# Queries and output gate as seven of eight block products, and the gates' tiles moved into the attention

## The chip, the core and the metric

The kernel runs on one core of one Trainium2 chip. Its metric is the device time of one execution in microseconds. The engines are named as in the profile: PE is TensorE (matmul), PEld its weight load, DVE VectorE, ACT ScalarE, POOL GpSimd, SP SyncE. SP and POOL each issue DMAs on a queue of their own.

## The reference

One layer of a hybrid encoder: 512 tokens, width 1024, float32. What bears on the change, with `rmsnorm(h)` the normalised input:

```python
h = rmsnorm(x, norm_mix_g)
gq, gk, gv, gr, glr, fq, fk, fv, ff, g_gla, g_fox = jnp.split(h @ w_in, IN_OFFSETS, axis=-1)
o_gla = gla_chunked(gq, gk, gv, log_a)                     # 4 heads of 128
o_gla = rmsnorm(o_gla, gla_out_norm_g) * silu(gr)          # output gate gr: 512 columns
fqh, fkh = rmsnorm(fq, fox_q_norm_g), rmsnorm(fk, fox_k_norm_g)   # 8 heads of 64
o_fox = fox_attention(fqh, fkh, fv, log_f)                 # causal softmax attention
y = sigmoid(g_gla + gate_b[0]) * (o_gla @ w_gla_branch) \
    + sigmoid(g_fox + gate_b[1]) * (o_fox @ w_fox_branch)
x = x + y @ w_out
a, val = jnp.split(rmsnorm(x, norm_ffn_g) @ w_up, 2, axis=-1)
return x + (gelu(causal_dwconv(a)) * val) @ w_down         # and a last rmsnorm
```

## The kernel before, in words

Every large product is made with float32 operands as a high and a low half: a piece of weights (128 x 1024) is loaded into a raw tile (`raw`, `rawz`, `rawp`, `rawx` by place), ACT casts it to `wh` (line 293), DVE makes `wl`, the difference (line 294), and PE runs three matmuls for each of its blocks: high by high, high by low, low by high (`mm3`, lines 328 to 330). Pieces are split three ahead of their use (`NW`). `recipes` is the list of pieces in order of use; `then` says what a split sets off: a plain load on SP's queue, or an accumulating load on POOL's queue, which adds a second block of weights to a raw tile. `COPY_AT` and `ADD_AT` hang DMAs in DRAM onto pieces: 24 copies and 24 accumulating additions that build sums of the down projection's blocks (`wsum`).

Some products are split in 2 x 2 blocks and made with seven block products instead of eight (numbered 1 to 7, in the order 5, 1, 3, 6, 2, 7, 4 or like it). Their weights are single blocks or sums of blocks, which the accumulating loads form: product 6 takes the raw tile of product 5 with a block added, 4 that of 6, 7 that of 3. In before this holds for keys and values (`fox_kv`, 14 half pieces of 12 matmuls, two steps each), the out product, the up and the down projection.

The stages, in order of PE: narrow products and the first sums, GLA's values (`vg`, 4 pieces), `fox_q` (4 pieces of 24 matmuls, 512 columns), `fox_kv`, with the steps of gated linear attention put between; then the forgetting attention; then eight branches; then out, up and down products.

Work that can be put between other work is a generator in `work`; `fill(n)` takes n steps of it. In the attention the generators are gate tiles (`gate_tile`): one step is one k of eight, three matmuls. There are 12 of them: 4 of the output gate (`zr`) and 8 of the first merge gate (`zg`). `FRONT` and `RUNS` set the order by hand: for each pair of units (`unit`: two heads and one or two blocks of queries) the logits are made (line 983), then a number is so many steps of gate tiles, `k` prepares keys and queries of the next two heads (`kh`, `kl`, `qh`, `ql`), `t` transposes a unit's probabilities (line 1017; ACT casts to `ph`, line 1023, DVE makes `pl`, line 1024), and `v` multiplies them with the values (line 1042). Behind the logits stand a DVE reduction (`ISA`, line 990), the exponential (ACT, line 995), the reciprocal and the scaling (ACT, line 997), then `t`.

The 8 tiles of the second gate (`zf`) alternate with the branches, two ahead (`GAHEAD`). A branch c is 24 matmuls (`pg` and `pf`), two sigmoids, two multiplies on DVE (lines 1157 and 1158), an addition on POOL (lines 1161 and 1168), and the making of the out product's operands (`o1`, `o7` for c < 4, `o65`, `o3`, `o24` for c >= 4), on ACT and DVE.

Of the kernel before, what the change touches and what calls it, by code (L numbers as in the profile page):

```python
# [53 lines left out]
GAHEAD = 2  # L54
# [39 lines left out]
def hybrid_kernel(ctx: ExitStack, tc, xT, xt, wp, wu, wd, wf, wn, pp, aw2, fing, out):  # L94
# [55 lines left out]
    at_pair = {}  # L150
    for p, r in PAIR:
        k11, k21, k12, k22 = (wps[i + r] for i in (12, 14, 8, 10))
        new, before, place = {
            1: (k11, None, "rawz"), 2: (k21, None, "rawz"), 3: (k22, None, "rawp"), 7: (k12, 3, None),
            5: (k12, None, "raw"), 6: (k22, 5, None), 4: (k21, 6, None),
        }[p]
        at_pair[p, r] = len(recipes)
        recipes.append((new, at_pair[before, r] if before else None, 1024, place))
# [519 lines left out]
    def fox_q():  # L678
        ssq = gpool.tile([P, NT, FH], F32, name="qssq")

        def done(tt, ps):
            nc.scalar.activation(out=qf[:, tt, :], in_=ps, func=AF.Copy, scale=rt[:, tt : tt + 1])
            squares(qf, ssq, tt)

        yield from token_group(xh, xl, done)
        qk_norm(qf, ssq, range(NT))

# [1129 lines left out]
```

## Time and profile before

| | |
|---|---|
| median of three runs | 688.78 us (688.37 to 690.36) |
| profiled execution | 688.75 us |
| its span | 687.0 us |
| mean granted clock of TensorE | 0.999 |
| DMA traffic | 142.23 MB, mean 207 GB/s |

Spans and starts are in microseconds from the start of the span. A row of the timeline has the start, the duration, engine, line, operation, what it writes and reads, and in brackets how long the engine was idle and what ended that. A row of the windows gives the busy time of each engine in that stretch, with the number of instructions, then the granted clock, the share of the 16 DMA engines that was busy and GB/s.

### The profile page before, as it was taken

How to read it: one execution, taken by the hardware profiler on the slowest of the kernel's cores; microseconds unless marked ns; L12 is line 12 of the kernel's file. 1: busy time of each engine (PE TensorE's matmuls, PEld its weight loads, DVE VectorE, ACT ScalarE, POOL GpSimd, SP SyncE). 2: the span in 40 equal slices, each digit the busy share in tenths (PEclk: the TensorE clock that was granted, in tenths of full speed). 3: DMA queues.
4: the chain of work that ended last, by engine and by line, in shares of the span. 5: the costliest groups of instructions: out<-in, count | busy, mean ns of one | idle time of the engine just before them, and what ended most of it. 6: DMA issues, size and time to landing. Idle time of an engine off the chain costs nothing.

```text
span 687.0 us, 10636 instructions
## 1 busy us (share of the span) xinstructions
PE 680.2 (99%) x3875; PEld 585.4 (85%) x3875; DVE 547.8 (80%) x856; ACT 430.9 (63%) x698; POOL 136.3 (20%) x196
## 2 busy tenths in 40 slices
PE   9999999999999999999999999999999999999996
PEld 6788888888888888888888999999999999888885
DVE  7774988858776767687679999888998889977884
ACT  8487676677767744344584956655666666655663
POOL 1125110122321424331210221121122111000222
PEclk9999999999999999999999999999999999999999
DMA  8769488989765489967975898999999988866643
GB/s 310 270 192 306 99 273 221 311 196 217 178 140 122 119 248 199 281 147 213 213 253 133 158 211 210 228 228 223 196 201 214 204 202 254 268 209 173 196 139 122
DMA packets 46184, 142.23 MB, mean 207 GB/s; under 512 B 5396, under 2 KB 9388, under 8 KB 46004
## 3 DMA queue, kind: packets, MB, share of 16 engines
q1 hardware_dynamic: 31156, 92.98, 40.3%
q0 software_dynamic: 11808, 43.52, 35.8%
q10 hardware_dynamic: 3168, 5.05, 2.1%
q8 instruction: 30, 0.49, 0.3%
q14 instruction: 22, 0.18, 0.1%
HBM read 137.32 MB, written 27.28 MB: 240 GB/s over the span
## 4 chain that ended last, share of the span: by engine, by line
PE 99%; ACT 0%; issue 0%; DVE 0%; ACTq 0%
PE ps_mm L328 21%; PE ps_mm L330 20%; PE ps_mm L329 20%; PE ps_wide L1463 8%; PE ps_wide L328 5%; PE ps_wide L329 5%; PE ps_wide L330 5%; PE ps_wide L1465 4%; PE ps_lg L1042 1%; PE ps_lg L983 1%; PE ps_pt L1017 1%; PE ps_mm L490 1%; PE ps_ax L328 1%; PE ps_ax L330 1%; PE ps_ax L329 1%; PE ps_ax L378 1%
## 5 line engine op out<-in xcount | busy, mean ns | idle before, releaser
L293 ACT CAST wh<-rawx 128x1024 fp32r<-128x1024 f32 x75 | 76.0, 1013 | 61.5 <-PE ps_mm L329 30.9
L328 PE MATMUL ps_mm<-xw,wh 128*128 128x512 f32 (+1 forms) x320 | 109.4, 342 | 0.2 <-ACT wh L293 0.2
L329 PE MATMUL ps_mm<-xw,wh 128*128 128x512 f32 (+1 forms) x320 | 107.8, 337 | 0.0
L330 PE MATMUL ps_mm<-xw,wl 128*128 128x512 f32 (+1 forms) x320 | 107.6, 337 | 0.0
L294 DVE TENSOR_TENSOR wl<-rawx,wh 128x1024 fp32r<-128x1024 f32 x75 | 88.3, 1179 | 13.8 <-ACT wh L293 13.8
L294 DVE TENSOR_TENSOR wl<-raw,wh 128x1024 fp32r<-128x1024 f32 x58 | 74.6, 1287 | 9.7 <-ACT wh L293 9.4
L293 ACT CAST wh<-raw 128x1024 fp32r<-128x1024 f32 x58 | 60.7, 1049 | 32.0 <-PE ps_mm L329 20.2
L328 PEld LDWEIGHTS ps_mm<-xw,wh 128*128 128x128 f32 x320 | 60.8, 190 | 7.8 <-issue 1.2
L330 PEld LDWEIGHTS ps_mm<-xw,wl 128*128 128x128 f32 x320 | 60.8, 190 | 6.5
L329 PEld LDWEIGHTS ps_mm<-xw,wh 128*128 128x128 f32 x320 | 60.8, 190 | 5.9 <-DVE xw L1252 0.2
L294 DVE TENSOR_TENSOR wl<-rawz,wh 128x1024 fp32r<-128x1024 f32 x31 | 39.2, 1266 | 16.7 <-ACT wh L293 16.4
L1463 PE MATMUL ps_wide<-xo,wh 128*128 128x512 f32 x192 | 48.1, 392 | 0.0
L301 POOL DMA_DIRECT2D rawx<-in_wu_dram x30 | 25.9, 865 | 104.6 <-DVE wl L294 68.6
L328 PE MATMUL ps_mm<-xc,wh 128*128 128x256 f32 (+1 forms) x136 | 45.1, 332 | 0.0
L329 PE MATMUL ps_mm<-xc,wh 128*128 128x256 f32 (+1 forms) x136 | 44.6, 328 | 0.0
L330 PE MATMUL ps_mm<-xc,wl 128*128 128x256 f32 (+1 forms) x136 | 44.5, 327 | 0.0
L293 ACT CAST wh<-rawz 128x1024 fp32r<-128x1024 f32 x31 | 32.4, 1044 | 14.2 <-issue 5.0
L1463 PEld LDWEIGHTS ps_wide<-xo,wh 128*128 128x128 f32 x192 | 34.6, 189 | 6.2
L328 PE MATMUL ps_mm<-wh,xw 128*128 128x512 f32 x96 | 37.7, 393 | 0.0
L329 PE MATMUL ps_mm<-wl,xw 128*128 128x512 f32 x96 | 37.4, 390 | 0.0
L330 PE MATMUL ps_mm<-wh,xw 128*128 128x512 f32 x96 | 37.4, 390 | 0.0
L309 POOL COPY tick<-wl 128x1 f32<-128x1 f32 x37 | 10.6, 286 | 134.5 <-DVE wl L294 134.5
(492 smaller groups left out, 1783.6 us busy)
## 6 DMA issues: line engine op xcount, KB each, us to landing
rawx<-in_wu_dram POOLq DMA_DIRECT2D x40, 512.0 KB, 7.1
rawz<-in_wp_dram SPq DMA_DIRECT2D x30, 512.0 KB, 4.6
raw<-in_wp_dram SPq DMA_DIRECT2D x22, 512.0 KB, 5.1
wsum<-in_wd_dram SPq DMA_DIRECT2D x20, 512.0 KB, 6.3
rawx<-in_wu_dram SPq DMA_DIRECT2D x20, 512.0 KB, 4.9
raw<-in_wu_dram SPq DMA_DIRECT2D x20, 512.0 KB, 5.5
rawx<-wsum SPq DMA_DIRECT2D x12, 512.0 KB, 4.0
wsum<-in_wd_dram POOLq DMA_DIRECT2D x10, 512.0 KB, 8.2
```

Source lines behind the costliest of these rows:

```text
L293: nc.scalar.copy(out=hi[:, :m], in_=raw[:, :m])
L294: last_split[:] = [nc.vector.tensor_sub(out=lo[:, :m], in0=raw[:, :m], in1=hi[:, :m].bitcast(F32))]
L301: nc.gpsimd.dma_start(raw, recipes[i][0], accum_op=ALU.add)
L309: now = nc.gpsimd.tensor_copy(out=tick, in_=lo[:, 0:1].bitcast(F32))
L328: mm(ps, lhsT=ah, rhs=bh, start=start, stop=False, **k)
L329: mm(ps, lhsT=ah, rhs=bl, start=False, stop=False, **k)
L330: mm(ps, lhsT=al, rhs=bh, start=False, stop=stop, **k)
L378: mm(warm, lhsT=nc.const_aps.tensor(1.0, (P, P), BF16), rhs=nc.const_aps.tensor(1.0, (P, T), BF16), start=True, stop=True,)
L490: mm(first[i], lhsT=w[:, i * P : (i + 1) * P], rhs=x, start=(k == j == 0), stop=False)
L983: last = mm(lg[:, place_of_q(qb)], lhsT=a[r, q], rhs=b[r, :n], start=(j == 0), stop=(j == 2))
L1463: mm(ps[:, i], lhsT=wh[:, c], rhs=both[p][:, k], start=first and k == 0, stop=False, skip_group_check=True)
L1465: mm(ps[:, i, 0], lhsT=wl[:, c], rhs=both[p][:, k, 0], start=False, stop=k == KH - 1, skip_group_check=True,)
```

## The change

Queries (`fq`) and output gate (`gr`) now are one pair of a seven-product stage, `pair_stage`, which also serves keys and values (with `PAIR2`, product 1 ahead of 5). The output gate so comes by token, not by feature: `silu` makes `gz` times its sigmoid and multiplies it into the normalised GLA output `ons`, which is transposed afterwards (`transpose_heads`, `HEADS_AT`). In place of `fox_q`, four tiles of the first gate (channels 2, 6, 3, 7) are made early, stored in DRAM (`early`) and loaded back as `zd` at the first branch. The attention is filled with the other four tiles of the first gate and all eight of the second; the numbers in `RUNS` sum to 80 instead of 88, and 8 steps are left behind the attention. The halves of `k1` and `k2` are made behind the next `ph` casts (`waiting`). The branches then run without gate tiles between them, in the order 0, 4, 1, 5, 2, 6, 3, 7; a branch is merged (`merge`) one branch later, and the last two additions are DVE's. Product 5 of the out product has raw tiles of its own (`five`), and the up stage's first sums are loaded earlier.

```diff
 RUNS = (
-    (6, "k1", 2, "t0", 6, "t1"),
-    (7, "t2", 4, "v0", 3, "t3"),
-    (6, "k2", 2, "t4", 6, "t5"),
-    (6, "v1", 1, "t6", 3, "k3", 4, "t7"),
-    (7, "t8", 4, "v2", 3, "t9"),
-    (8, "t10", 6, "t11", 4, "v3"),
+    (6, "k1", 1, "t0", 4, "t1"),
+    (5, "t2", 5, "v0", 3, "t3"),
+    (6, "k2", 2, "t4", 5, "t5"),
+    (6, "v1", 1, "t6", 3, "k3", 3, "t7"),
+    (5, "t8", 5, "v2", 3, "t9"),
+    (8, "t10", 5, "t11", 4, "v3"),
 )
-GAHEAD = 2
+NEARLY = 4
+ORDER = (0, 4, 1, 5, 2, 6, 3, 7)
+GG = ORDER[KD - NEARLY :] + ORDER[: KD - NEARLY]
+HEADS_AT = (6, 8)
+NORM_AT = (5, 1)
...
-COPY_AT = [10 + i for i in range(24)]
-ADD_AT = [32 + i if i < 10 else 42 + (i - 10) * 20 // 14 for i in range(24)]
+COPY_AT = [8 + i * 2 // 3 for i in range(18)] + [20 + i // 2 for i in range(6)]
+ADD_AT = list(range(42, 56)) + [59, 61, 63, 64]
+LAST_ADD_AT = [2 + 3 * i for i in range(6)]
...
-OSUM = (1, 3)
+OSUM = (3, 4)
+PAIR2 = PAIR[2:4] + PAIR[:2] + PAIR[4:]
...
+    at_qr = pair_recipes(20, 8, ("rawz", "rawp", "raw"), PAIR)
+    at_kv = pair_recipes(16, 12, ("rawz", "raw", "rawp"), PAIR2)
...
+        behind(at_qr[7, r], "load", at_kv[5, r])
+        behind(at_qr[2, 1] + r, "sum", at_kv[5, r], at_kv[1, r])
...
+    def put_early(i):
+        def put(ps):
+            tag = ("sq", "sq", "fsq", "gls")[i]
+            z = gpool.tile([P, T], F32, tag=tag, name="early", bufs=2 if tag == "sq" else 1)
+            nc.vector.tensor_mul(out=z, in0=ps, in1=rb)
+            nc.sync.dma_start(early[:, i], z)
+
+        return put
...
+    def silu(tt):
+        gz, ons = late["gz"], late["ons"]
+        sg = gpool.tile([P, 512], F32, tag="sq", name="sg", bufs=2)
+        nc.scalar.activation(out=sg, in_=gz[:, tt], func=AF.Sigmoid)
+        nc.vector.tensor_mul(out=sg, in0=gz[:, tt], in1=sg)
+        nc.vector.tensor_mul(out=ons[:, tt], in0=ons[:, tt], in1=sg)
...
-    work += [fox_q(), fox_kv()]
-    fill(4)
+    work += [gate_tile(put_early(i)) for i in range(NEARLY)] + [
+        pair_stage(PAIR, qssq, qf, lambda: late["gz"], silu)
+    ]
+    fill(8)
...
+    fill(18)
+    work += [pair_stage(PAIR2, kssq, kf, lambda: vf)]
+    for u in range(2):
+        fill(HEADS_AT[u])
+        transpose_heads(u)
     fill()
...
-    gates = [gate_tile(z) for z in zr + zg]
+    gates = [gate_tile(put_in(z)) for z in [zg[c] for c in GG[NEARLY:]] + [zf[c] for c in ORDER]]
...
             if what[0] == "k":
-                prepare_k(n)
-                prepare_q(n)
+                waiting.append(prepare(n))
+                if n == 3:
+                    waiting.pop()()
             elif what[0] == "t":
                 for j in range(2):
                     transposed(2 * units[n][0] + j, units[n][1])
+                while waiting:
+                    with tc.issue_after(last_copy[0].ins):
+                        waiting.pop()()
...
+    for i, c in enumerate(ORDER):
+        w = piece()
+        pg, pf = pmm(), pmm()
...
+        if i == 0:
+            for j, n in enumerate(GG[:NEARLY]):
+                zg[n] = bpool.tile([P, T], F32, tag="zd", name="zd", bufs=NEARLY)
+                nc.sync.dma_start(zg[n], early[:, j])
+        z = zf[c]
+        sigmoid(zg[c], zg[c], bias=col(C_GB + c))
+        last_sigmoid = sigmoid(z, z, bias=col(C_GB + KD + c))
+        if i > 0:
+            merge(ORDER[i - 1])
+        nc.vector.tensor_mul(out=zg[c], in0=pg, in1=zg[c])
+        nc.vector.tensor_mul(out=z, in0=pf, in1=z)
+        add_branches(c, nc.gpsimd if i < KD - 2 else nc.vector)
+        if i in HELD:
+            held.append(piece())
+    merge(ORDER[-1])
```

On DVE, in the attention's first run, before: from the reciprocals of the second unit to the reduction of the third (`rs` a reciprocal, `kl` and `ql` low halves of keys and queries, `zr` a gate tile's multiply, `pl` the low halves of two units' transposed probabilities, one after `t0` and one after `t1`).

```order
L996 RECIPROCAL rs<-rs 128x1 x4
L949 TENSOR_TENSOR kl<-ps_lg,kh 128x512
L959 SCALAR_TENSOR_TENSOR ql<-ps_lg,gqs,qh 128x512
L934 TENSOR_TENSOR zr<-ps_mm,rb 128x512
L294 TENSOR_TENSOR wl<-rawz,wh 128x1024
L1024 TENSOR_TENSOR pl<-ps_pt,ph 128x384 x2
L1024 TENSOR_TENSOR pl<-ps_pt,ph 128x3x128 x2
L990 ISA pr,nm<-ps_lg,cb_616 128x512
```

The same place after (the gate tile is `zg` now; line numbers are those of the changed file):

```order
L1036 RECIPROCAL rs<-rs 128x1 x6
L1064 TENSOR_TENSOR pl<-ps_pt,ph 128x384 x2
L996 TENSOR_TENSOR kl<-ps_lg,kh 128x512
L998 SCALAR_TENSOR_TENSOR ql<-ps_lg,gqs,qh 128x512
L976 TENSOR_TENSOR zg_1688<-ps_mm,rb 128x512
L307 TENSOR_TENSOR wl<-rawz,wh 128x1024
L1064 TENSOR_TENSOR pl<-ps_pt,ph 128x3x128 x2
L1030 ISA pr,nm<-ps_lg,cb_620 128x512
```

The two `pl` of `t0` moved ahead of `kl`, `ql`, the multiply and `wl`, which now stand between them and the two of `t1`; the reduction still is behind the latter.

On DVE in the branches, before: from a gate tile's multiply with `rb` to the next (a branch with c >= 4, whose operands `ol` and `s` are made at once).

```order
L934 TENSOR_TENSOR zf<-ps_mm,rb 128x512
L294 TENSOR_TENSOR wl<-raw,wh 128x1024
L1157 TENSOR_TENSOR zg_1388<-ps_mm,zg_1388 128x512
L1158 TENSOR_TENSOR zf<-ps_mm,zf 128x512
L294 TENSOR_TENSOR wl<-rawz,wh 128x1024
L1170 TENSOR_TENSOR zg_1384<-zf,zg_1384 128x256
L1121 TENSOR_TENSOR ol_3129<-zf,oh_2620 128x512
L1124 SCALAR_TENSOR_TENSOR zg_1384<-zg_1384 128x256
L1124 SCALAR_TENSOR_TENSOR s<-zf,zg_1384 128x256
L1121 TENSOR_TENSOR ol_2619<-zg_1384,oh_2618 128x512
L1121 TENSOR_TENSOR ol_2617<-s,oh_2616 128x256
L934 TENSOR_TENSOR zf<-ps_mm,rb 128x512
```

After, from the multiplies of one branch with c >= 4 to those of the next (`zr` and `zg` hold the second gate's tiles as well, `zd` the early ones):

```order
L1228 TENSOR_TENSOR zg_1690<-ps_mm,zg_1690 128x512
L1165 TENSOR_TENSOR ol_2914<-ps_ax,oh_2913 128x256
L1229 TENSOR_TENSOR zr<-ps_mm,zr 128x512
L307 TENSOR_TENSOR wl<-rawz,wh 128x1024
L1200 TENSOR_TENSOR zg_1689<-zr,zg_1689 128x256
L1165 TENSOR_TENSOR ol_3165<-zr,oh_2919 128x512
L1168 SCALAR_TENSOR_TENSOR zg_1689<-zg_1689 128x256
L1228 TENSOR_TENSOR zd<-ps_mm,zd 128x512
L1168 SCALAR_TENSOR_TENSOR ps_ax<-zr,zg_1689 128x256
L1165 TENSOR_TENSOR ol_2918<-zg_1689,oh_2917 128x512
L1165 TENSOR_TENSOR ol_2916<-ps_ax,oh_2915 128x256
L1229 TENSOR_TENSOR zg_1691<-ps_mm,zg_1691 128x512
```

The gate tile's multiply and its `wl` are gone from between; the merge of a branch is now mixed with the multiplies of the branch that follows.

On POOL at the pair stages, before: the accumulating loads of products 6, 7 and 4 (two halves each), and then the first additions into `wsum`, each behind a copy of one column (`tick`).

```order
L301 DMA raw<-in_wp_dram 128x1024 x2
L301 DMA rawp<-in_wp_dram 128x1024 x2
L301 DMA raw<-in_wp_dram 128x1024 x2
L309 COPY tick<-wl 128x1
L311 DMA wsum_69<-in_wd_dram 128x1024
L309 COPY tick<-wl 128x1
L311 DMA wsum_69<-in_wd_dram 128x1024
```

After:

```order
L314 DMA raw<-in_wp_dram 128x1024 x2
L314 DMA rawp<-in_wp_dram 128x1024 x2
L314 DMA raw<-in_wp_dram 128x1024 x2
L322 COPY tick<-wl 128x1
L324 DMA rawp<-in_wp_dram 128x1024
L322 COPY tick<-wl 128x1
L324 DMA rawp<-in_wp_dram 128x1024
L314 DMA rawp<-in_wp_dram 128x1024 x2
L314 DMA raw<-in_wp_dram 128x1024 x2
L314 DMA rawp<-in_wp_dram 128x1024 x2
L322 COPY tick<-wl 128x1
L324 DMA wsum_69<-in_wd_dram 128x1024
```

Behind the loads of the first pair stage now come eight of the second (`rawp` and `raw`), the first two of them behind a `tick`, and only then the additions into `wsum`.

More of the change, by code (lines that the diff above doesn't have):

```diff
@@ L149, in hybrid_kernel, with pair_recipes @@
     recipes += [(w, None, 1024, "raw" if i < 2 else "rawz") for i, w in enumerate(wps[:8])]
[L150 to L158, printed above, removed]
+    def pair_recipes(a, b, places, pair):
+        at = {}
+        for p, r in pair:
+            k11, k21, k12, k22 = (wps[i + r] for i in (a, a + 2, b, b + 2))
+            new, before, place = {
+                1: (k11, None, places[0]), 2: (k21, None, places[0]), 3: (k22, None, places[1]), 7: (k12, 3, None),
+                5: (k12, None, places[2]), 6: (k22, 5, None), 4: (k21, 6, None),
+            }[p]
+            at[p, r] = len(recipes)
+            recipes.append((new, at[before, r] if before else None, 1024, place))
+        return at
+    at_qr = pair_recipes(20, 8, ("rawz", "rawp", "raw"), PAIR)
+    at_kv = pair_recipes(16, 12, ("rawz", "raw", "rawp"), PAIR2)
     at_out = {}
-    n_out = 16 + GH + 3 * KD
+    n_gate = 24
+    n_out = n_gate + 3 * KD - NEARLY
     o11, o21, o12, o22 = (wps[n_out + 2 * i : n_out + 2 * i + 2] for i in range(4))
@@ L573, in hybrid_kernel @@
         )
-    vg = gpool.tile([P, NT, 512], F32, name="vg")
+    vg = gpool.tile([P, NT, 512], F32, tag="vg", name="vg")
+    early = dpool.tile([P, NEARLY, T], F32, name="early")
     last_v = []
@@ L676, in qk_norm, with gate_tile @@
             )
[L678 to L686, printed above, removed]
+    def gate_tile(put):
+        ps = pmm()
+        wh, wl = piece()
+        for k in range(KD):
+            c = slice(k * P, (k + 1) * P)
+            mm3(ps, wh[:, c], wl[:, c], xh[k], xl[k], k == 0, k == KD - 1)
+            yield
+        put(ps)
+    def put_early(i):
[5 more added lines that the diff above has]
+        return put
     for k in range(KD):
@@ L735, in pair_operand, with pair_stage @@
         return xh[j * K2 + k][:, t], xl[j * K2 + k][:, t]
-    def fox_kv():
-        ssq = gpool.tile([P, NT, FH], F32, name="kssq")
-        banks = {}
-        for p, r in PAIR:
+    def pair_stage(pair, ssq, left, right, final=lambda tt: None):
+        banks = {name: [pmm() for _ in range(2)] for name in "zx"}
+        for p, r in pair:
+            if left is kf and (p, r) == NORM_AT:
+                with tc.issue_after(last_split[0].ins):
+                    qk_norm(qf, qssq, range(NT))
             name = {5: "z", 3: "z", 1: "x", 2: "x", 6: "y", 7: "y", 4: "y"}[p]
@@ L847, in hybrid_kernel @@
     for tt in range(NT):
-        fill(2)
+        fill(4 if tt < NT - 1 else 2)
         for c in range(2 * tt, min(2 * tt + 2, NC - 1)):
@@ L890, in hybrid_kernel @@
                 )
+    late["gz"] = gpool.tile([P, NT, 512], F32, tag="vg", name="gz")
     for u in range(2):
@@ L1267, in hybrid_kernel @@
     out_product(5, accz)
-    for t2 in range(2):
-        nc.vector.tensor_add(out=x2[t2][0], in0=x2[t2][0], in1=ox[t2])
-    minus(1, 1, accz)
     accx = [pax(), pax()]
-    out_product(2, accx)
+    out_product(2, accx, rs=(0,))
+    with tc.issue_after(last_split[0].ins):
+        minus(1, 1, accz)
+    out_product(2, accx, rs=(1,))
+    with tc.issue_after(last_split[0].ins):
+        for t2 in range(2):
+            nc.vector.tensor_add(out=x2[t2][0], in0=x2[t2][0], in1=ox[t2])
     finish_block(0, 0, accx, nc.vector.tensor_add)
```

283 lines of the change are left out of this document (141 added, 142 removed).

## The prediction

> **What bounds the kernel now.** I read the page first: shares, slices, chain.
>
> ```profile
> span 687.0 us, 10636 instructions
> PE 680.2 (99%) x3875; PEld 585.4 (85%) x3875; DVE 547.8 (80%) x856; ACT 430.9 (63%) x698; POOL 136.3 (20%) x196
> PE   9999999999999999999999999999999999999996
> PE 99%; ACT 0%; issue 0%; DVE 0%; ACTq 0%
> ```
>
> The chain that ended last is 99% TensorE, and PE is busy in every slice but the last. So each matmul that goes is worth its own time, and each wait newly put on PE costs its own time; nothing else counts. The profiled execution took 688.75 us, 1.75 us more than its span and 0.03 us under the median of 688.78, so I reckon from 688.75. Less than about 0.3% (2.07 us) can't be told from no change here: faster means under 686.7, slower over 690.85.
>
> A busy PE may still be a slow one, so next I look at the spacing of matmuls in one block of 24 (a branch, which is as large as a gate tile), by the timeline.
>
> ```profile
> 241.26 0.39 PE L328 MATMUL ps_mm<-ogh,wh 128*128 128x512 f32 x1
> ...
> 246.47 0.39 PE L330 MATMUL ps_mm<-oth,wl 128*128 128x512 f32 x1
> 246.70 0.39 PE L328 MATMUL ps_mm<-xw,wh 128*128 128x512 f32 x1
> ```
>
> Start to start, 24 matmuls take 246.70 - 241.26 = 5.44 us, 0.2267 us each, though one is drawn as 0.39 us: they overlap, and the spacing is the price. Three of them (one step of a gate tile, one k) are 0.68 us. Then the other engines by stretches of 20 us:
>
> ```profile
> core 0: us, PE busy (x) PEld busy (x) DVE busy (x) ACT busy (x) POOL busy (x), PEclk, DMA share, GB/s
> 20.00:40.00 20.00, 20.00 (x103) 15.89 (x96) 14.27 (x30) 11.73 (x17) 1.03 (x3) 1.00 0.66 238
> 40.00:60.00 20.00, 20.00 (x94) 16.68 (x93) 11.38 (x10) 17.21 (x22) 11.88 (x14) 1.00 0.76 219
> 60.00:80.00 20.00, 20.00 (x159) 16.36 (x158) 16.64 (x23) 12.03 (x16) 2.06 (x5) 1.00 0.65 203
> 80.00:100.00 20.00, 20.00 (x161) 17.21 (x160) 19.18 (x47) 14.32 (x46) 2.14 (x3) 1.00 0.77 230
> 100.00:120.00 20.00, 20.00 (x96) 16.51 (x95) 16.59 (x28) 12.28 (x19) 2.13 (x3) 1.00 0.86 216
> 260.00:280.00 20.00, 20.00 (x90) 16.57 (x89) 12.78 (x18) 7.63 (x11) 9.53 (x14) 1.00 0.98 234
> 400.00:420.00 20.00, 19.82 (x136) 18.35 (x136) 19.31 (x27) 12.47 (x18) 3.64 (x5) 1.00 0.94 211
> ```
>
> The granted clock is 1.00 everywhere. PE has no hole up to the up stage; at 400 to 420 it lacks 0.18 us. DVE and the DMA engines are the ones with little room in places.
>
> **The change part by part.**
>
> *Matmuls that go.* Queries (4 token pieces) and output gate (4 feature pieces) were 8 x 24 = 192 matmuls of 512 columns. As seven of eight block products they are 14 half pieces of 12, 168. 24 x 0.2267 = -5.44 us, all of it on PE, hence on the path. Branches, gates and out products keep their counts.
>
> *Less to fill the attention with.* This is the dearest part. In the attention PE covers the softmax chains with gate tile steps. Before, 12 tiles gave 96 steps; now 88 lie in the attention, and the cover of the chain that ends at `t2` and `t8` falls from 7 steps to 5, that between `t0` and `t1` from 6 to 4. How much of that cover was spare I read from one run of before:
>
> ```profile
> 145.47 0.82 PE L1017 MATMUL ps_pt<-ident,pr 128*128 128x128 f32 x6
> 152.71 1.03 PE L1017 MATMUL ps_pt<-ident,pr 128*128 128x128 f32 x8
> 156.55 0.47 PE L1042 MATMUL ps_lg<-pl,v 128*128 128x512 f32 x1
> 141.29 0.69 DVE L949 TENSOR_TENSOR kl<-ps_lg,kh 128x512 fp32r<-128x512 f32 x1 [1.32 <-ACT kh L948]
> 143.16 1.21 DVE L294 TENSOR_TENSOR wl<-rawz,wh 128x1024 fp32r<-128x1024 f32 x1
> 146.51 1.02 DVE L1024 TENSOR_TENSOR pl<-ps_pt,ph 128x384 fp32r<-128x384 f32 x2 [1.20 <-ACT ph L1023]
> 147.45 0.68 DVE L990 CUSTOM_DVE_ANT_0 pr<-ps_lg,cb 128x512 f32<-128x512 f32 x1
> 155.78 1.28 DVE L1024 TENSOR_TENSOR pl<-ps_pt,ph 128x512 fp32r<-128x512 f32 x2
> 142.69 0.85 ACT L1023 CAST ph<-ps_pt 128x384 fp32r<-128x384 f32 x2
> 149.60 1.32 ACT L997 ACTIVATE pr<-pr,rs 128x512 f32<-128x512 f32 x2
> 153.57 1.03 ACT L293 CAST wh<-rawz 128x1024 fp32r<-128x1024 f32 x1
> ```
>
> `t2` (152.71) transposes probabilities that were scaled by 150.92: 1.8 us to spare. Its chain began with the DVE reduction at 147.45, 1.98 us after `t1` (145.47), right behind the `pl` that DVE had idled for. Now DVE comes later: between `t0` and `t1` lie only 0.45 + 4 x 0.68 = 3.2 us, and DVE must do in them `pl` of `t0` (which waits for `ph`, 0.85), `kl`, `ql`, a gate tile's multiply (some 0.6 each, start to start) and a `wl` (1.1). With ACT free at 140.8, the two `pl` of `t0` end near 142.6, the four others near 145.5, the `pl` of `t1` near 146.5, while `t1` stands at 143.2. So the reduction begins 3.3 us after `t1`, 1.3 later than before, and the transposes come 2 x 0.68 = 1.36 us earlier: 1.8 - 1.3 - 1.36 = -0.9, a wait of 0.9 us. It can be 0 (if DVE gets `wl` behind the `pl`, 1.1 us come back), or 2 (if DVE loses as much again to a late load). I take 0.9, and the same for `t8`, which stands behind the same gap with the same 5 steps: +1.8. For `v0` and `v2` I take nothing: in before the last `pl` came at the very moment its product was due (first half done about 156.4, product at 156.55), but a `wh` (1.03) and a `wl` sat ahead of `ph` and `pl` there; both now stand behind, and there are 5 steps instead of 4. The halves of `k1` and `k2` now wait for the `ph` casts, so `ql` reaches the third unit's logits late: I allow 0.5 us in all, between 0 and 1.4 (one `ph` and one `ql`). Attention: +2.3, between 0 and 5.4 (2 x 2 + 1.4).
>
> *The two pair stages.* 14 pieces of 12 matmuls (2.72 us each) come twice in a row, and with them eight accumulating loads each, in place of eight plain ones. What a load costs of the 16 DMA engines follows from the DMA view of 85 to 140 us, where the first pair stage of before ended:
>
> ```profile
> q1 hardware_dynamic: 3445, 11.61, 60.5%
> q0 software_dynamic: 778, 2.79, 27.7%
> wsum<-in_wd_dram SPq DMA_DIRECT2D x11, 512.0 KB, 6.1
> rawp<-in_wp_dram POOLq DMA_DIRECT2D x2, 512.0 KB, 7.0
> DMA to landing us min/median/max: 7.0/7.4/10.0
> ```
>
> A plain 512 KB takes 0.605 x 55 / 11.61 x 0.524 = 1.5 us of all engines, an accumulating one 0.277 x 55 / 2.79 x 0.524 = 2.9. (The last row is of the tile `rawp`.) From 20 to 120 us the engines were busy 74 of 100 us by the windows. The copies into `wsum` now start at the 8th piece and run closer, some 8 more before 120 us (12 us), four `early` tiles of 256 KB go out (3 us), and one pair stage takes the place of the other: 89 of 100. That is dense but no bound. Between the splits of products 5 and 6 of the kv pair there are now 4 pieces (10.9 us) instead of 6; a piece is split 3 pieces (8.2 us) ahead of its use, and the add lands 7 to 10 us after its issue, with a `wh` and a `wl` (2.3) behind it: 19.1 - 12.3 = 6.8 us to spare. I take 0, between 0 and 2.
>
> *POOL and DVE in the branches.* Gate tiles no longer stand between the branches, so what DVE does per 10.88 us must be done per 5.44. And POOL's additions block it:
>
> ```profile
> 247.67 1.29 POOL L1161 TENSOR_TENSOR zg<-zf,zg 128x512 f32<-128x512 f32 x1 [1.10 <-DVE zf L1158]
> 247.80 2.25 DVE L294 TENSOR_TENSOR wl<-raw,wh 128x1024 fp32r<-128x1024 f32 x1 [0.21 <-ACT wh L293]
> 249.97 0.41 DVE L1121 TENSOR_TENSOR ol<-zg,oh 128x256 fp32r<-128x256 f32 x1
> 250.31 0.41 DVE L1164 TENSOR_TENSOR s<-zg 128x256 f32<-128x256 f32 x1
> 257.63 1.22 DVE L294 TENSOR_TENSOR held<-raw,held 128x1024 fp32r<-128x1024 f32 x1 [3.16 <-ACT held L293]
> 258.77 0.68 DVE L1157 TENSOR_TENSOR zg<-ps_mm,zg 128x512 f32<-128x512 f32 x1
> 259.38 0.68 DVE L1158 TENSOR_TENSOR zf<-ps_mm,zf 128x512 f32<-128x512 f32 x1
> ```
>
> Start to start a 256 wide difference is 0.34 us, a 512 wide one 0.61, a `wl` 1.14; beside a POOL addition the `wl` took 2.25, 1.03 more. A branch c < 4 is 2 x 0.61 + 1.14 + 3 x 0.34 = 3.4 us of DVE, c >= 4 is 4 x 0.61 + 1.14 + 4 x 0.34 = 4.9. Eight: 33.2; two held pieces 2.3; two additions on DVE 1.2; six POOL additions 6 x 1.03 = 6.2: 42.9 us, and PE gives 8 x 5.44 = 43.5. DVE fits barely, and the late merges of the last two branches feed product 5, behind product 1. I take 0, between 0 and 1.5.
>
> Here the Trainium skill, SBUF — State Buffer, "SBUF: two separate sides", speaks against the change: GpSimd and VectorE hold their shared pair of ports exclusively for a whole instruction, and any DVE operation with two SBUF inputs is shut out. By that rule an addition would cost DVE its whole 1.29 us, as an estimate 44.4 of 43.5 us, and the sum would be 0.9 us higher; the trace shows the lock (2.25 beside 1.22) but 1.03 us of it, and I stay with the row.
>
> *The rest.* Six more `wh`, `wl` pairs, four `sg` multiplies and two table loads (one at the first silu, one ahead of the first exponential) lie on ACT and DVE in the kv pair, where ACT had 12 to 14 of 20 us busy: 0. Preloading the up stage's first sums can give back the 0.18 us of 400 to 420 at most: -0.2 if its DMAs are then early, 0 if not; I take -0.1. The tail is not touched.
>
> Sum: 688.75 - 5.44 + 2.3 - 0.1 = 685.5 us.
>
> **The rivals.** *All hidden.* DVE takes the casts in a kinder order than I think, and `t2` and `t8` find their probabilities. For it: 1.1 us of my 1.3 us delay is one `wl`, which depends on when its load lands. Then 688.75 - 5.44 - 0.2 = 683.1, or 684.1 if one wait of a us is left. *The chains eat the gain.* In all six runs of the attention a transposition or a product waits, not in two: six at 0.9 are 5.4 us, against -5.5: 688.6, no change. Against it: the gaps at `t5`, `t7`, `t11` shrink by one step (0.68), not by two, and 1.8 us were spare where I looked. *The loads are late (the slower case).* If the 89 of 100 us are more, because accumulating loads of two pairs and the copies collide, PE stands at the qr and kv pairs until the data is there. PE waits once an add takes over 10.0 + 6.8 = 16.8 us from issue to landing, and each further us costs one at three products of both pairs; it decides at 17.7 us (6 x 0.9 = 5.4 on top of 685.5 is 690.9), and 18 us give 685.5 + 6 x 1.2 = 692.7. For it: DMA at 0.98 in the branches of before. Against: PE did not wait there.
>
> **How the numbers follow.** Chances: attention waits of 1.2 to 3.5 us as summed 0.47 (684.4 to 686.7); all hidden 0.24 (682.8 to 684.4); eaten by the chains 0.17 (686.7 to 690.85); late loads 0.12 (above 690.85). Faster 0.71, same 0.17, slower 0.12. The range leaves out the slower case and a little of the upper end of the third: 682.8 to 690.2.
>
> **What would show it.** The matmuls of `ps_mm` 24 fewer and spaced 0.2267 us; PE waits on ACT `pr` at the second and fifth run, near 0.9 us each, and none at `v0`; no wait of PE on `wl` in the pair stages; DVE busy over 19 of 20 us in the branches with `wl` of over 2 us beside POOL additions. The prediction is wrong if PE shows waits for `wh` or `wl` behind a DMA ahead of the attention, or if the branches' DVE work reaches product 5 late by more than 1.5 us.

## The result, and the profile after

The changed kernel takes 685.21 us (median of six, 684.81 to 685.57); the kernel before, on the same chip, 688.83 (median of six, 688.35 to 690.36). The ratio is 0.9945, with a 95% interval of 0.9932 to 0.9958: faster by 0.55%. The profiled execution took 685.57 us, so beside the 688.75 of before the traces have 3.18 us to explain.

The profile page of after, its span, busy times and chain:

```profile
span 683.9 us, 10635 instructions
PE 675.7 (99%) x3851; PEld 580.3 (85%) x3851; DVE 550.0 (80%) x870; ACT 442.8 (65%) x712; POOL 147.1 (22%) x199
PE 74%; DVE 8%; DMA 7%; ACT 6%; issue 4%; POOL 0%; SPq 0%; DVEq 0%; POOLq 0%; ACTq 0%
```

There are 3851 matmuls, 24 fewer, and PE is as full as before. The chain nevertheless fell from 99% PE to 74%. That is no measure of what was lost: a wait of any length sends the chain from PE to whatever released it, and it stays on the other engines until it meets PE again. The waits themselves (waits of PE in after: what PE did next, what ended the wait, us, times, longest) are short:

```profile
PE ps_ax L391 <- PEq L1866: 0.9, 1, 0.9
PE ps_pt L1057 <- ACT pr L1037: 0.7, 1, 0.7
PE ps_ax L920 <- DVE prev L889: 0.3, 1, 0.3
PE ps_mm L342 <- DVE wl L307: 0.2, 1, 0.2
```

The first stands in before as well. The second is new and stands in the repetition of after too: transpositions that wait for scaled probabilities. The last two don't.

To see where the 3.18 us arose I compare starts of the same instruction in both traces: the first `ps_lg` (start of the attention), the last product with `v` in it, the last row of the branches that multiplies high by high, the first `ps_wide` (start of the up stage), the last matmul. "Lost" is what a stretch took beyond its matmuls.

| stretch | before | after | expected from the matmuls alone | lost |
|---|---|---|---|---|
| up to the attention | 129.10 | 167.24 | 129.10 + 14 x 2.72 = 167.18 | 0.06 |
| attention | 95.65 | 92.15 | 95.65 - 8 x 0.68 = 90.21 | 1.94 |
| branches | 86.55 | 48.48 | 86.55 - 7 x 5.44 = 48.47 | 0.01 |
| up to the up stage | 65.20 | 65.18 | 65.20 | -0.02 |
| up and down stage | 304.41 | 304.55 | 304.41 | 0.14 |

In all 24 x 0.2267 = 5.44 us were saved and 2.1 lost, nearly all of that in the attention; the last matmul so starts 3.3 us earlier, and 0.1 to 0.2 us went behind it. One trace does not settle a few tenths: the kernels below that share after's first stretch begin the attention between 167.09 and 167.81, and most of their up and down stages take 304.02 to 304.06. The attention of after is 92.15 here and 92.12 in the repetition. The timeline of after around `t0`, `t1` and `t2` shows how (chosen rows of ACT, DVE and PE in order of time; before's counterparts are in the prediction):

```profile
171.89 1.28 ACT L1035 ACT_TABLE_LOAD   x1
...
175.36 0.80 ACT L1037 ACTIVATE pr<-pr,rs 128x128 f32<-128x128 f32 x2 [0.94 <-DVE rs L1036]
...
180.38 1.02 DVE L1064 TENSOR_TENSOR pl<-ps_pt,ph 128x384 fp32r<-128x384 f32 x2 [1.21 <-ACT ph L1063]
181.32 0.68 DVE L996 TENSOR_TENSOR kl<-ps_lg,kh 128x512 fp32r<-128x512 f32 x1
181.57 0.82 PE L1057 MATMUL ps_pt<-ident,pr 128*128 128x128 f32 x6
181.92 0.74 DVE L998 SCALAR_TENSOR_TENSOR ql<-ps_lg,gqs,qh 128x512 fp32r<-128x512 f32 x1
182.58 0.68 DVE L976 TENSOR_TENSOR zg<-ps_mm,rb 128x512 f32<-128x512 f32 x1
183.18 1.36 DVE L307 TENSOR_TENSOR wl<-rawz,wh 128x1024 fp32r<-128x1024 f32 x1
184.46 1.01 DVE L1064 TENSOR_TENSOR pl<-ps_pt,ph 128x384 fp32r<-128x384 f32 x2
185.39 0.68 DVE L1030 CUSTOM_DVE_ANT_0 pr<-ps_lg,cb 128x512 f32<-128x512 f32 x1
187.54 1.32 ACT L1037 ACTIVATE pr<-pr,rs 128x512 f32<-128x512 f32 x2
188.30 1.27 PE L1057 MATMUL ps_pt<-ident,pr 128*128 128x128 f32 x8 [0.69 <-ACT pr L1037]
```

DVE has no idle time in brackets from 181.32 on: `kl`, `ql`, the gate's multiply, `wl` and `pl` stand in front of the reduction, which starts 185.39 - 181.57 = 3.82 us behind `t1`, where before it was 1.98. The scaling comes so late that `t2` waits. Against the normal spacing (before's, less 0.68 us for each step that went), `t2` lost 1.08 us (0.85 ahead of it, 0.23 between its own transpositions), `t8` 0.35, `v0` 0.36 and `v2` 0.19: 1.98, which is the 1.94 of the table. A part of the lateness is older than `t0`: at 175.36 ACT waited 0.94 us for `rs`. In this order all six reciprocals stand behind all six reductions, where before two of the six stood between the reductions.

The windows of after in the pair stages and in the branches (columns as in the prediction: stretch, busy time of each engine, granted clock, DMA share, GB/s):

```profile
60.00:80.00 20.00, 20.00 (x159) 16.36 (x158) 17.15 (x23) 9.96 (x12) 3.79 (x4) 1.00 0.96 336
80.00:100.00 20.00, 19.74 (x159) 16.86 (x158) 13.57 (x31) 11.61 (x41) 2.27 (x3) 1.00 0.97 296
100.00:120.00 20.00, 20.00 (x90) 16.57 (x89) 15.56 (x18) 12.16 (x14) 4.16 (x7) 1.00 0.97 227
265.00:308.50 43.50, 43.50 (x193) 36.03 (x192) 32.82 (x56) 23.07 (x37) 19.21 (x19) 1.00 0.85 222
```

The DMA engines were nearly full through the pair stages, yet PE did not wait for a load. In the branches DVE was busy 32.82 of 43.5 us and PE all of them.

### The profile page after: what moved, and what is told of

It reads as the page before. It is cut to its first block, busy times and chain, and to the rows that moved or that the text cites. A ratio compares the mean times of both kernels' runs of the same rounds, so it can differ in the third digit from the quotient of the medians.

```text
span 683.9 us, 10635 instructions
## 1 busy us (share of the span) xinstructions
PE 675.7 (99%) x3851; PEld 580.3 (85%) x3851; DVE 550.0 (80%) x870; ACT 442.8 (65%) x712; POOL 147.1 (22%) x199
## 4 chain that ended last, share of the span: by engine, by line
PE 74%; DVE 8%; DMA 7%; ACT 6%; issue 4%; POOL 0%; SPq 0%; DVEq 0%; POOLq 0%; ACTq 0%
PE ps_mm L341 15%; PE ps_mm L342 15%; PE ps_mm L343 15%; PE ps_wide L1521 8%; PE ps_wide L1523 4%; PE ps_wide L341 3%; PE ps_wide L342 3%; PE ps_wide L343 3%; DMA rawx<-in_wu_dram 3%; DVE wl L307 2%; DMA xo<-x2d 2%; DMA cb<-nct 2%; ACT wh L306 1%; PE ps_lg L1082 1%; ACT pr L1035 1%
## 5 line engine op out<-in xcount | busy, mean ns | idle before, releaser
L341 PE MATMUL ps_mm<-xw,wh 128*128 128x256 f32 (+1 forms) x296 | 100.2, 338 | 0.0
L342 PE MATMUL ps_mm<-xw,wh 128*128 128x256 f32 (+1 forms) x296 | 98.5, 333 | 0.0
L343 PE MATMUL ps_mm<-xw,wl 128*128 128x256 f32 (+1 forms) x296 | 98.2, 332 | 0.0
L307 DVE TENSOR_TENSOR wl<-raw,wh 128x1024 fp32r<-128x1024 f32 x58 | 71.6, 1235 | 14.3 <-ACT wh L306 14.0
L341 PEld LDWEIGHTS ps_mm<-xw,wh 128*128 128x128 f32 x296 | 56.3, 190 | 7.0 <-issue 1.0
L343 PEld LDWEIGHTS ps_mm<-xw,wl 128*128 128x128 f32 x296 | 56.2, 190 | 5.6
L342 PEld LDWEIGHTS ps_mm<-xw,wh 128*128 128x128 f32 x296 | 56.3, 190 | 5.0 <-DVE xw L1305 0.2
L322 POOL COPY tick<-wl 128x1 f32<-128x1 f32 x39 | 19.2, 493 | 128.2 <-DVE wl L307 112.1
L341 PE MATMUL ps_mm<-xc,wh 128*128 128x256 f32 (+1 forms) x128 | 42.1, 329 | 0.0
L342 PE MATMUL ps_mm<-xc,wh 128*128 128x256 f32 (+1 forms) x128 | 41.5, 324 | 0.0
L343 PE MATMUL ps_mm<-xc,wl 128*128 128x256 f32 (+1 forms) x128 | 41.4, 323 | 0.0
L342 PE MATMUL ps_mm<-wl,xw 128*128 128x512 f32 x88 | 34.4, 390 | 0.2 <-DVE wl L307 0.2
L341 PE MATMUL ps_mm<-wh,xw 128*128 128x512 f32 x88 | 34.3, 389 | 0.0
L343 PE MATMUL ps_mm<-wh,xw 128*128 128x512 f32 x88 | 34.2, 389 | 0.0
```

The costliest lines, as they stand in the source:

```text
L307: last_split[:] = [nc.vector.tensor_sub(out=lo[:, :m], in0=raw[:, :m], in1=hi[:, :m].bitcast(F32))]
L322: now = nc.gpsimd.tensor_copy(out=tick, in_=lo[:, 0:1].bitcast(F32))
L341: mm(ps, lhsT=ah, rhs=bh, start=start, stop=False, **k)
L342: mm(ps, lhsT=ah, rhs=bl, start=False, stop=False, **k)
L343: mm(ps, lhsT=al, rhs=bh, start=False, stop=stop, **k)
```

## The experiments

All but one start from the kernel after. Ratios are against the kernel before, timed on the same chip.

**Was it the number of steps that cover the chains?** Theory one says that DVE's queue makes the reduction late; the rival is that 88 steps in place of 96 are too few. First, before with after's `RUNS`, nothing else changed.

> The kernel before with the changed kernel's numbers in RUNS and nothing else: 8 of its 96 steps now come behind the attention, the work is the same. If fewer steps in the attention are by themselves what cost 2.0 us, it takes 688.8 + 2.0 = 690.8 us (between 690 and 691.5), with waits at t2 and t8. Rival: the waits come from the rest of the change (the halves of keys and queries behind ph, other loads); then it stays at 688.8.

Measured: 689.41 us, ratio 1.0007 (0.9996 to 1.0019). The attention took 90.66 us, 0.45 over 90.21, and no wait of PE is listed in it. The timeline of this kernel at `t1`:

```profile
143.47 0.82 PE L1017 MATMUL ps_pt<-ident,pr 128*128 128x128 f32 x6
146.18 0.69 DVE L990 CUSTOM_DVE_ANT_0 pr<-ps_lg,cb 128x512 f32<-128x512 f32 x1
```

The reduction is 2.71 us behind `t1`, not 3.82, and the time is nearer to the rival's 688.8 than to 690.8. So the fewer steps are by themselves worth 0.45 of the 1.94 us, and they cost it at `t8` and `v2`: `t2` stands 5.88 us behind `t1`, which is 7.24 less the two steps, and loses nothing. What `t2` and `v0` lost in after needs the other parts of the change.

Next the steps were given back to after, at the waiting places:

```diff
-    (5, "t2", 5, "v0", 3, "t3"),
+    (7, "t2", 5, "v0", 3, "t3"),
-    (5, "t8", 5, "v2", 3, "t9"),
+    (7, "t8", 5, "v2", 3, "t9"),
```

> The changed kernel with 7 steps instead of 5 ahead of t2 and of t8; the four steps come from the eight behind the attention, so the work is the same. If the 2.0 us that the attention lost are the softmax chains of t2 and t8 and what they delay (v0, v2), all of it comes back: the waits of 1.1 and 0.35 us vanish, those ahead of v0 and v2 (0.3 and 0.2) too, and the time is 685.2 - 1.9 = 683.3 us (ratio to before 0.992). Rival: the steps behind the attention covered the start of the branches; with four fewer PE waits there for the first branch's operands, and the time stays at 685.

Measured: 686.95 us, ratio 0.9965 (0.9953 to 0.9978), 1.7 us slower than after. The waits of PE, and DVE's timeline ahead of `v0`:

```profile
PE ps_mm L342 <- DVE held L1181: 1.2, 1, 1.2
PE ps_lg L1082 <- DVE pl L1064: 0.9, 1, 0.9
```

```profile
193.36 1.23 DVE L307 TENSOR_TENSOR wl<-rawz,wh 128x1024 fp32r<-128x1024 f32 x1 [1.51 <-ACT wh L306]
194.50 1.28 DVE L1064 TENSOR_TENSOR pl<-ps_pt,ph 128x512 fp32r<-128x512 f32 x2
```

`t2` and `t8` wait no more. But two steps more put a tile's end ahead of `t2`, and with it a piece to be split: `wl` now stands ahead of the `pl` that `v0` needs. The expectation missed that. And with four steps fewer behind the attention the first branch stands still for a low half of the GLA output, which is kept in the tile `held` (L1181). That is the rival of the expectation, and with the wait at `v0` it cost more than the 685 us allowed. The same with two steps more between `t0` and `t1` and between `k3` and `t7`:

```diff
-    (6, "k1", 1, "t0", 4, "t1"),
+    (6, "k1", 1, "t0", 6, "t1"),
-    (6, "v1", 1, "t6", 3, "k3", 3, "t7"),
+    (6, "v1", 1, "t6", 3, "k3", 5, "t7"),
```

> The changed kernel with 6 steps instead of 4 between t0 and t1, and 5 instead of 3 between k3 and t7; t2 and t8 keep their 5. Theory one, DVE's queue: the reduction of t2 starts late because kl, ql, a gate multiply and wl stand between the two pl; with 1.36 us more room it starts 1.36 us nearer to t1 (2.4 to 2.5 us behind it instead of 3.8), and the wait at t2 falls from 1.1 us to 0: 683.8 to 684.2 us. Theory two, plain cover: 5 steps behind t1 are too few whatever DVE does; then the waits at t2 and t8 stay and the time stays at 685.2.

Measured: 687.41 us, ratio 0.9975 (0.9966 to 0.9983). The waits of PE have moved to the products and to the branches, and below them `t1` and the reduction in the timeline:

```profile
PE ps_lg L1082 <- DVE pl L1064: 1.4, 2, 0.9
PE ps_mm L342 <- DVE held L1181: 1.2, 1, 1.2
```

```profile
182.91 0.82 PE L1057 MATMUL ps_pt<-ident,pr 128*128 128x128 f32 x6
185.22 0.68 DVE L1030 CUSTOM_DVE_ANT_0 pr<-ps_lg,cb 128x512 f32<-128x512 f32 x1
```

The time fits neither theory, but the mechanism is that of theory one: the reduction comes 2.31 us behind `t1`, and `t2` waits no more. It did not come earlier, though. Counted from the first `ps_lg` it starts at 18.00 us, as in the repetition of after (18.00; 18.15 in the trace above): DVE's queue sets when it starts, and only `t1` was moved.

Both edits together put all 88 steps in the attention:

> The changed kernel with both of these edits: all eight gate steps in the attention, none behind it. If the attention's waits are all that can come back, the time is that of the first edit alone, 683.3 us, since the waits are gone already. Rival: the tile behind the attention covered the split of the GLA output and of the last head pair for the first branch; then PE waits 1 to 4 us for otl or ogl ahead of branch 0, and the time is 684.5 to 687.

Measured: 689.02 us, ratio 0.9995 (0.9982 to 1.0008): the whole gain is gone. The wait of PE, then the windows around it:

```profile
PE ps_mm L341 <- ACT oth L1100: 2.2, 1, 2.2
```

```profile
267.00:268.00 1.00, 0.30 (x1) 0.29 (x1) 0.32 (x1) 1.00 (x3) 0.00 (x0) 0.81 1.06 434
268.00:270.00 2.00, 1.86 (x4) 0.73 (x4) 1.13 (x2) 2.00 (x4) 0.00 (x0) 0.50 0.90 299
274.00:275.00 1.00, 1.00 (x4) 0.79 (x4) 0.00 (x0) 0.00 (x0) 0.00 (x0) 0.78 0.99 336
```

There is no wait in the attention any more. But the first branch waits 2.2 us for `oth`, a high half of the attention's outputs, and from the end of that wait the granted clock is 0.50 for some 6.8 us (0.38 + 6.0 + 0.44 by the windows). The eight steps that after leaves behind the attention cover that. More cover is thus no cure: it moves a wait, and takes cover from the next place.

**What makes the chain late?** First the order of the halves. After makes them behind the `ph` casts; here `k1` and `k2` make them at once, as before:

```diff
-                if n == 3:
-                    waiting.pop()()
+                waiting.pop()()
```

> The changed kernel with the halves of k1 and k2 made where they are prepared, as in the kernel before, not behind the next ph; all numbers of steps as they are. Theory one, DVE's queue: in the kernel before with 88 steps, where kl and ql stand ahead of the pl of t0, the reduction came 2.7 us behind t1 instead of 3.8; so here too, and the wait at t2 goes from 1.1 to 0.1 us or less: 684.1 to 684.3 us, ratio 0.993. Theory two, plain cover (5 steps are too few): the wait stays, 685.2. Rival three: t0's ph is late behind kh and qh, and t4 or the logits of k2 wait instead, 685.2 or more.

Measured: 685.07 us, ratio 0.9945 (0.9932 to 0.9957), the time of after. The wait of PE:

```profile
PE ps_pt L1057 <- DVE pl L1064: 0.6, 1, 0.6
```

Theory one's 684.2 us did not come. `t2` waits for nothing that the list shows, but `t1`, at 182.93, does: the order in the queue decides who waits, its length that somebody does. The reduction starts 18.11 us behind the first `ps_lg`, as in after, so the new place of the halves is not what makes it late. So two instructions were taken out of DVE's queue, the `wl` between `t0` and `t1` and that ahead of `t7` (the splits 48 and 53), and given to POOL:

```diff
+            eng = nc.gpsimd if n in (48, 53) else nc.vector
-            last_split[:] = [nc.vector.tensor_sub(...)]
+            last_split[:] = [eng.tensor_sub(...)]
```

> The changed kernel with the two wl differences that stand between t0 and t1 and between k3 and t7 made by POOL instead of DVE; nothing else. Theory one, DVE's queue between t0 and the reduction: it gets shorter by 1.1 to 1.3 us, so the reduction comes 2.6 us behind t1 instead of 3.8, the waits at t2 (1.1) and t8 (0.35) go, and those ahead of v0 and v2 (0.35 and 0.2), which ACT passed on from the same reduction, with them: 685.2 - 1.4 to 2.0 = 683.2 to 683.8 us. Theory two, plain cover: no change at t2, 685.2. Rival: POOL is late with it (its masks and DMA issues stand behind) and shuts DVE out: 686 or more.

Measured: 683.08 us, ratio 0.9914 (0.9902 to 0.9927). This beats both kernels. The timeline:

```profile
184.50 0.68 DVE L1031 CUSTOM_DVE_ANT_0 pr<-ps_lg,cb 128x512 f32<-128x512 f32 x1
...
186.23 2.40 POOL L308 TENSOR_TENSOR wl<-rawz,wh 128x1024 fp32r<-128x1024 f32 x1
```

The reduction starts 2.54 us behind `t1` (181.96), the attention takes 89.89 us, and PE waits nowhere in it. All of the 1.94 us are back and 0.3 more, for two `wl` that take POOL 2.40 and 2.64 us in place of DVE's 1.22. Then the nine splits 46 to 54 on POOL, to see how far that goes:

> The changed kernel with all nine wl differences of the attention made by POOL. If only the two between t0 and t1 and ahead of t7 matter, the time is that of the run with two, 683.2 to 683.8 us; if POOL, at 2.5 us or more for each, holds up masks for the reductions or accumulating loads, PE waits there instead and it is 684 to 687.

Measured: 689.8 us, ratio 1.0008 (0.9994 to 1.0022). The waits of PE:

```profile
PE ps_mm L344 <- POOL wl L308: 2.2, 1, 2.2
PE ps_lg L990 <- DVE kf L693: 1.9, 1, 1.9
```

```profile
166.11 3.45 DVE L693 TENSOR_TENSOR kf<-kf,rq 128x512 f32<-128x512 f32 x2
166.41 2.61 POOL L308 TENSOR_TENSOR wl<-raw,wh 128x1024 fp32r<-128x1024 f32 x1 [0.50 <-ACT wh L306]
```

That is more than either time of the expectation. Where PE needs a `wl` soon, POOL's 2.4 us come too late. And a `wl` on POOL holds up DVE: the two multiplies of `kf` take 1.29 us in after and 3.45 here, beside POOL's `wl`, and PE waits for them. So the cure only works where the piece has time and where no urgent DVE work stands beside it. The profiled execution took 687.63 us, one of the shorter of twelve (687.11 to 691.45); what the longer ones lost beyond these two waits this trace does not show.

Last, the late start of the chain. Three reductions of the first softmax are issued behind the reciprocals of earlier pieces, so that four reciprocals stand between the reductions (two in before, none in after); the other rows of DVE's queue keep their places:

```diff
+                at = {(1, 0): (0, 0), (1, 1): (0, 1), (0, 2): (1, 0)}.get((h, qb))
+                with tc.issue_after(recips[at]) if at else ExitStack():
                     nc.vector.tensor_tensor_reduce(
...
-                nc.vector.reciprocal(out=rs, in_=rs)
+                recips[h, qb] = nc.vector.reciprocal(out=rs, in_=rs).ins
```

> The kernel after, but in the first softmax of the attention the reductions of the second head and of the third block of queries are issued behind the reciprocals of the pieces before them, as in the kernel before; the queues are otherwise those of after. Theory one (the late softmax at the start is a part of the wait at t2): ACT no longer waits 0.94 us for rs, the last scaling of the second unit ends about 0.9 us nearer to the attention's first matmul, the two pl of t0 and with them the whole DVE queue up to the reduction move by as much, the reduction begins about 2.9 us behind t1 and not 3.8, and t2 waits about 0.2 us and not 1.08: 685.2 - 0.9 = 684.3. Theory two (only the DVE work between t0 and t1 counts, which the start does not move): the queue between t0 and the reduction is as long as before, the wait at t2 stays at 0.9 to 1.1, 685.1 to 685.3. If the table load of the exponential sets the start alone, ACT waits for it in either case and nothing moves: 685.2.

Measured: 684.18 us, ratio 0.9935 (0.9921 to 0.9948). Its timeline:

```profile
178.54 0.62 ACT L1039 ACTIVATE pr<-pr,rs 128x384 f32<-128x384 f32 x1 [0.23 <-DVE rs L1038]
184.41 0.68 DVE L1032 CUSTOM_DVE_ANT_0 pr<-ps_lg,cb 128x512 f32<-128x512 f32 x1
187.32 1.27 PE L1059 MATMUL ps_pt<-ident,pr 128*128 128x128 f32 x8
```

The last scaling ends 12.07 us behind the first `ps_lg` (167.09), in after 12.75, before 11.70. The reduction is 2.99 us behind `t1` (181.42), `t2` has no wait in brackets, and the attention takes 90.96 us, 1.19 less than after. Counted from the first `ps_lg`, the reduction starts at 17.32 us here, at 16.87 in wl_on_pool_two and at 17.04 in before_with_88, whose start is not late, against 18.00 to 18.15 in after. So an earlier start gives back 1.2 of the 1.94 us and a shorter queue all of them. They are two cures of one lateness, not shares of a sum, and the two together were not tried.

**Is a matmul worth its time?** Product 7 is left out of the query and gate pair, 24 matmuls more:

```diff
+                    if p == 7 and left is qf:
+                        continue
```

> The changed kernel without the 24 matmuls of product 7 in the query and gate pair (part of the computation is left out; its loads, casts and everything else stay). It asks what the next 24 matmuls there would be worth. If TensorE alone bounds the pair stages: 685.2 - 5.4 = 679.8 us (ratio 0.987). If the loads are the next bound, because the DMA engines are at 0.96 to 0.98 from 60 to 140 us, PE waits for wh or wl of later pieces and less comes: 681 to 685.

Measured: 683.2 us, ratio 0.9914 (0.9901 to 0.9928): 2 us less than after, not 5.4. The wait of PE and the windows behind it:

```profile
PE ps_mm L342 <- DVE wl L307: 1.9, 1, 1.9
```

```profile
112.00:113.00 1.00, 0.00 (x0) 0.00 (x0) 1.00 (x3) 0.53 (x1) 0.00 (x0) 1.00 0.77 270
114.00:115.00 1.00, 1.00 (x5) 0.77 (x5) 0.86 (x1) 1.00 (x2) 0.91 (x1) 0.83 0.91 315
115.00:116.00 1.00, 1.00 (x4) 0.81 (x3) 0.59 (x1) 0.78 (x2) 0.15 (x1) 0.50 0.89 209
```

DVE is busy in every us from 109 to 114, so here it is DVE that the pair stages next run against, not the loads; then the clock is 0.50 for 3.4 us. The attention begins only 1.4 us earlier. The 24 matmuls of the change itself were worth their whole time because the pieces left still hid DVE's work.

**Could the loads have been late?** The copies hang on the pieces they hung on before:

```diff
-COPY_AT = [8 + i * 2 // 3 for i in range(18)] + [20 + i // 2 for i in range(6)]
+COPY_AT = [10 + i for i in range(24)]
```

> The changed kernel with the 24 copies in DRAM hung on pieces 10 to 33, one each, as before. If the transfers are dense but hidden, the time is unchanged (685.2) though the DMA share from 60 to 120 us falls below 0.9. If the early, dense copies cost the pair stages something, it falls by up to 0.3 us; if the late ones collide with the accumulating loads of the kv pair, PE waits for wl there and it rises by 1 to 4 us.

Measured: 686.34 us, ratio 0.9958 (0.9943 to 0.9974). A wait of PE, and ACT's timeline ahead of it:

```profile
PE ps_mm L341 <- ACT kf L785: 1.2, 1, 1.2
```

```profile
141.38 1.05 ACT L306 CAST wh<-rawp 128x1024 fp32r<-128x1024 f32 x1 [2.99 <-DMA rawp<-in_wp_dram]
142.33 1.26 ACT L785 ACTIVATE kf<-ps_mm,rt 128x512 f32<-128x512 f32 x2
```

With the copies later, the DMA share from 120 to 140 us is 1.05. An accumulated load is late: it is issued at 132.61 and lands 8.7 us later, where in after the same load is issued at 130.87 and lands 5.8 us later. ACT stands 2.99 us at its cast, and PE waits, not for that weight but for the `kf` behind it on ACT. The attention starts 1.35 us later than in after. So the mechanism of the slower rival exists, with 1.1 us and not 5 or more; the earlier copies kept it away.

**POOL's additions.** All eight on POOL, in place of six:

> The changed kernel with the last two branch additions on POOL too, as the other six. By the rows an addition takes 2.2 us there when a wl starts with it, against 0.6 on DVE; the last branch's operands then reach product 5 (behind product 1) up to 1.6 us later. If that product has no room left, the time rises by 0.5 to 1.6 us; if it has, it stays at 685.2.

Measured: 686.32 us, ratio 0.9962 (0.9949 to 0.9976), 1.1 us slower than after, in two waits of PE behind the branches:

```profile
PE ps_mm L341 <- DVE x2t L1261: 0.6, 1, 0.6
PE ps_ax L342 <- DVE wl L307: 0.5, 1, 0.5
```

So the two last additions on DVE are worth about 1 us. The timeline of after shows what such an addition does to DVE within the branches:

```profile
278.27 1.22 DVE L307 TENSOR_TENSOR wl<-rawz,wh 128x1024 fp32r<-128x1024 f32 x1
278.44 2.20 POOL L1188 TENSOR_TENSOR zr<-zr,zg 128x512 f32<-128x512 f32 x1 [0.53 <-DVE zr L1229]
280.68 0.43 DVE L1200 TENSOR_TENSOR zg<-zr,zg 128x256 f32<-128x256 f32 x1 [1.19 <-POOL zr L1188]
```

Before, the addition came first and the `wl` was drawn out to 2.25 us; here the `wl` comes first, keeps its 1.22, and the addition is drawn out from 1.29 to 2.20. DVE then idles for the result. The Trainium skill, SBUF — State Buffer, "SBUF: two separate sides", says that whichever of the two starts first has the shared ports for its whole instruction; the rows agree to 0.14 us: 278.27 + 1.22 = 279.49, and 1.29 ahead of the addition's end at 280.64 is 279.35.

**A repetition.** After once more, beside the two kernels with `wl` on POOL:

> The changed kernel itself beside them on the same chip, as the measure for differences of a few tenths of a per cent: 685.2 us, ratio 0.9945.

Measured: 685.09 us, ratio 0.9945 (0.9933 to 0.9957), the attention 92.12 us. The medians that differ by 1 and 2 us above are thus well outside of what a repetition moves (0.12 us).

## Why the prediction was right

The forecast was 685.5 us, the median is 685.21. By its steps:

- *Matmuls, -5.44.* Right: 24 fewer, and every stretch outside the attention shortened or lengthened by its matmuls to within 0.14 us.
- *Attention, +2.3.* Measured +1.94. The mechanism at `t2` was the one named, with 0.9 predicted and 1.08 found. But the sum came near in part by luck: `t8` lost 0.35 and not 0.9; `v0` and `v2` lost 0.36 and 0.19 where I took nothing; the halves cost nothing of their own at the third unit's logits, where I allowed 0.5.
- *`t8`, "behind the same gap".* That reading was wrong. Ahead of `t7` lie six steps (3, `k3`, 3), one fewer than before, and not four. The reduction there is 3.05 us behind `t7`, where before it was 3.18, so it is no later; what changed for `t8` is its cover, 5 steps in place of 7, and before_with_88 loses about as much there (0.45 with `v2`).
- *Why the chain is late.* The step "with ACT free at 140.8" failed. I carried over the start of the chain from before and looked only at what stands between `t0` and `t1`. The changed order of the reciprocals, which the order of the DVE queue already showed (`rs` x6 in one row), let ACT idle; reciprocals_between gets 1.2 of the 1.94 us back there. The reduction came 3.82 us behind `t1` (3.67 in the repetition), where I had 3.3. Without the late start it is 2.71 (before_with_88), so I had reckoned the queue itself 0.6 too long.
- *The 1.8 us to spare at `t2`.* They were counted to the end of two scalings. In after `t2` starts at 188.30, while the row of the two scalings ends at 187.54 + 1.32 = 188.86: the start needs only the first. With the reduction at 3.82 my sum would have given a wait of 1.4; that it came out at 1.08, near 0.9, is two errors that cancel.
- *Table loads, 0.* The load itself is hidden: ACT starts it at 171.89 and afterwards still waits 0.26 us for DVE. It was not tried whether its place has a part in the changed order.
- *Pair stages, 0.* Right (0.06, in a stretch that moves by some tenths from trace to trace), and the DMA share came as summed: the five windows from 20 to 120 us hold 0.72, 0.83, 0.96, 0.97 and 0.97, that is 89 of 100 us. But the 6.8 us to spare were too many. In after the load issued at 130.87 has landed 5.8 us later and its cast begins at 139.34, 2.7 us behind that. In copies_as_before PE waited with a landing of 8.7 us, where by my sum only one over 16.8 would have mattered: ACT, which stood at the cast, held back the `kf` behind it, and I had not followed ACT's order of work.
- *Branches, 0.* Right in time, wrong in the picture: I had DVE busy for 42.9 of 43.5 us and over 19 of 20; the window shows 32.82. Merges run past the branches, and the time beside a POOL addition shows as idle time of DVE and as a longer addition, not as a longer `wl`.
- *Up stage, -0.1.* Not to be settled. The wait of 0.18 us for a `wh` in before (416.62) is gone, but PE waited 0.2 us for a `wl` in the down stage, and the two stages took 0.14 us longer; in the repetition of after they took 304.04, 0.37 less than before. before_with_88, which loads no sums earlier, takes 304.02 and has no such wait either.

Of the rivals, "all hidden" (683.1) is what wl_on_pool_two reaches with two instructions moved. "The chains eat the gain" came about in all_88_in, by another way: not six waits in the attention but one behind it, and the clock.

## What to carry to other kernels

When matmuls cover a chain on other engines, first count the instructions that stand in the queue ahead of the chain's next link, and look where the chain starts; only then count the steps of cover. Here two instructions moved to a less busy engine (POOL, 22% of the span) gave back what eight steps of cover could not. Before cover is moved, look at what it covers now and where the next weight's split will fall. And a split moved to a slower engine pays only where its result has the time, and where it does not hold up an urgent instruction of the engine that it leaves.

## What the runs showed of the hardware that was not expected

A short wait of PE can cost more than itself. After 1.9 us without a matmul in skip_24 the granted clock was 0.50 for 3.4 us (from 0.9 us behind the end of the wait), and after 2.2 us in all_88_in for 6.8 us, with matmuls of 512 columns 0.43 us apart in both. It is not certain to happen: wl_on_pool_all waited 2.24 us at 234.7 and kept 1.00 in its profiled execution, and of the twelve executions of all_88_in the mean granted clock was 0.993 in seven (688.9 to 690.7 us) and 0.996 to 0.999 in five (686.9 to 688.6 us). The Trainium skill, TensorE: Matmul & The Clock Gate, "Part 1: The HAM clock gate (the "warmup" mystery)", has the clock halved after at least one idle window of about 3.4 us, the window running freely. The half clock agrees, the length of the wait does not: here 1.9 us were enough. The 3.4 and 6.8 us at half clock are once and twice that window. That it depends on where in a window the wait falls would fit the twelve executions, but no run tested it.
